# A third weight load split behind another step, and a norm's small products moved up by three and six products

## The chip, the cores and the metric

The kernel runs on one core of a Trainium2 chip. The metric is the device time of one execution in microseconds (us), the median of several. TensorE (PE) does matrix products, VectorE (DVE) and ScalarE (ACT) element-wise work, GpSimd (POOL) a little of it, and SyncE (SP) issues most of the DMA transfers.

## The reference

One transformer block over 512 tokens of width 1024, all in float32, batch and depth 1:

```
h  = rmsnorm(x)
z  = h @ W_in      # MLA q-latent 256 | MLA kv-latent 128 | rope key 32 | diff q, k, v 512 each
x += concat[8 MLA heads x 64, 4 differential heads x 128] @ W_out
x += W_down( silu(causal_dwconv3(h2 W_gate)) * (h2 W_up) ),   h2 = rmsnorm(x), width 2816
x += sigmoid(rmsnorm(x) W_pg) * (p W_pp)                       # p: 512 x 256
```

A differential head subtracts two softmax maps: `attn = probs[0] - lam * probs[1]`, each with a relative-position bias added to its logits. Attention is causal by chunks of 64 tokens.

## The kernel before

**Products.** Every product is three TensorE products, since a float32 number is split in a rounded high half and a low rest: `mm3` (L152 to L157) runs high by high (L155), high weight-low (L156 or L157), and low by high. Every weight is therefore loaded raw (`load_raw`, L140, by SyncE's queue), cast by ScalarE into its high half (L148) and subtracted by VectorE into its low half (L149); `load_w` does all three, and there are three raw buffers in the attention part. A raw buffer is free for the next load when the subtraction has read it.

**Order.** TensorE's instructions run in the order in which the code writes them. VectorE's and ScalarE's are placed by the framework's scheduler in the attention part, and in the order of the code from the FFN's preparation on (`region`, a manual schedule of VectorE, ScalarE and GpSimd). `tc.issue_after(ins)` tells the scheduler to put a block's VectorE instructions behind `ins`.

**Attention.** The MLA heads end in four outputs `yT0` to `yT3` (pairs of heads, 128 x 512), which `y_split` turns into `yh` (ScalarE, L183) and a low rest `yh0l` to `yh3l` (VectorE, L184); `df["ysplit"]` is the last such subtraction. W_out comes in tiles `o{kq}{dq}`: kq is 0 for the MLA half of its rows and 1 for the differential half, dq the quarter of its columns. `wo_units` feeds the MLA half's products between the differential heads' steps and adds each to x (L631). A differential step (`diff_logits`) writes logits `dl{head}{row block}{map}` to a bank (heads, blocks and maps counted from 0); VectorE adds the bias and takes the row minimum (L675), ScalarE takes the exponential with its sum (L676), and VectorE combines the two maps: a reciprocal (L680), the factor `cf` (L681), the map `pmd` (L682). At a head's end `mo` (L702) reads all four row sums.

**Between attention and FFN.** The last products of W_out end in x; its squares are summed by ScalarE, GpSimd and VectorE. TensorE meanwhile projects p in eight blocks (`pp_unit`, six products each). `norm_r` sums the squares over the rows with four tiny products (L925), takes the power -1/2 on GpSimd and writes a diagonal matrix on VectorE (L928); `norm_b` broadcasts it by one product (nrb, L932) that ScalarE copies (L933). From there `tokens` scales x into the FFN's input, one block `xg0` to `xg7` at each `next(tk)`: VectorE scales (L996) and subtracts the block ahead of it (L998), ScalarE casts (L1000). `pp_out` copies a block of p's projection out of its bank (ScalarE, L948) and sends it to DRAM. Each `next(w1)` prepares one weight of the FFN's second tile (cast L835, subtraction L839); the first tile's gate product `g0` takes the bank of the tag "tp" after `pp5`, and `u0` one of the tag "lg".

Of the kernel before, what the change touches and what calls it, by code (L numbers as in the profile page):

```python
# [21 lines left out]
T = 512  # L22
# [72 lines left out]
def hybrid_block(ctx: ExitStack, tc: tile.TileContext, a: dict, out: bass.AP):  # L95
# [13 lines left out]
    def bank(tag, name):  # L109
        return pp_.tile([P, 512], F32, tag=tag, bufs={"acc": 2, "lg": 3, "tp": 2, "ob": 1}[tag], name=name)  # L110
# [32 lines left out]
    def load_w(src, n, name, eng=None):  # L143

        raw = load_raw(src, n, name)
        hi = wp["pool"].tile([P, 1024], F32R, tag="hi", bufs=wp["w"], name=f"hi_{name}")
        lo = wp["pool"].tile([P, 1024], F32R, tag="lo", bufs=wp["w"], name=f"lo_{name}")
        S.copy(hi[:, :n], raw[:, :n])  # L148
        (eng or V).tensor_tensor(lo[:, :n], raw[:, :n], _f32(hi[:, :n]), op=ALU.subtract)  # L149
        return hi, lo  # L150

    def mm3(ps, blocks, first=True, last=True, again=False):  # L152
        n = len(blocks)
        for i, (xh, xl, wh, wl) in enumerate(blocks):
            TE.matmul(ps, xh, wh, start=first and i == 0, stop=False, skip_group_check=again)  # L155
            TE.matmul(ps, xh, wl, start=False, stop=False, skip_group_check=again)  # L156
            TE.matmul(ps, xl, wh, start=False, stop=last and i == n - 1, skip_group_check=again)  # L157

    def rms(y, ss, n, width):

        m = sm.tile([P, 32], F32, tag="rs_m", name="rs_m")[:, :n]
        V.tensor_scalar(m, ss, 1.0 / width, EPS, op0=ALU.mult, op1=ALU.add)
        G.tensor_tensor(y, m, mhalf[:, :n], op=ALU.pow)
# [84 lines left out]
    for kq in range(4):  # L248
# [12 lines left out]
        for j in range(2):  # L261
            k = 2 * kq + j
# [217 lines left out]
    for t in range(NT):  # L480
        kv_ = kvb[:, t]
        sqk = sq_tile("sqk")[:, :H * 64].rearrange("p (h d) -> p h d", d=64)
        for c in range(2):
            hs = slice(4 * c, 4 * c + 4)
            ps = bank(UP_BANKS[(2 * t + c) % 4], f"ukv{t}{c}")
# [18 lines left out]
    for t in range(NT):  # L504
        q_ = xn_tile(f"qn{t}")[:, :H * QK].rearrange("p (h d) -> p h d", d=QK)
        sq = sq_tile("sqq")[:, :H * QK].rearrange("p (h d) -> p h d", d=QK)
        for c in range(2):
            hs = slice(4 * c, 4 * c + 4)
            ps = bank(UP_BANKS[(2 * t + c) % 4], f"uq{t}{c}")
# [101 lines left out]
    yh, yl, df = [None] * 8, [None] * 8, {}  # L611
# [9 lines left out]
    def wo_blocks(k0, k1, b, w):  # L621

        c = [slice((k % 4) * 256 + (b % 2) * P, (k % 4) * 256 + (b % 2) * P + P) for k in range(k0, k1)]
        return [(w[0][:, c[i]], w[1][:, c[i]], yh[k0 + i], yl[k0 + i]) for i in range(k1 - k0)]
# [5 lines left out]
    def add_x(b, ps):  # L630
        V.tensor_tensor(xb(b), xb(b), ps, op=ALU.add)  # L631
# [3 lines left out]
    def wo_w(kq, dq):  # L635
        if (kq, dq) in wo_first:
            return wo_first.pop((kq, dq))
        return load_w(a["w_out"][kq, dq], 1024, f"o{kq}{dq}")

    def wo_units(kq, dqs, nk):  # L640

        for dq in dqs:
            w = wo_w(kq, dq)
            if kq:
                wo2[dq] = w
            for b in (2 * dq, 2 * dq + 1):
                ps = bank("acc", f"o{kq}{b}")
                for k in range(0, nk, 2):
                    mm3(ps, wo_blocks(4 * kq + k, 4 * kq + k + 2, b, w), k == 0, k == nk - 2)
                    if k == nk - 2:  # L650
                        add_x(b, ps)
                    yield
# [158 lines left out]
    ptw, wpp = (pk[:, 0], pk[:, 1]), [(pk[:, 2], pk[:, 3])]  # L811
# [90 lines left out]
    for b in order:  # L902
        if b in early:
            ps = early[b]
            mm3(ps, wo_blocks(7, 8, b, wo2[b // 2]), False, True)
        else:
            ps = bank("tp" if b == 3 else "lg", f"o3{b}")
# [13 lines left out]
    def norm_r():  # L921

        ss, ps = nrm["ss"], bank("ob", "nr")
        for t in range(NT):
            TE.matmul(ps[:, t:t + 1], ss[:, tsl[t]], ones[:, :1], start=True, stop=True)  # L925
        r4 = sm.tile([P, NT], F32, tag="r4", name="r4")
        rms(r4, ps[:, :NT], NT, D)
        V.tensor_tensor(nrm["dg"].rearrange("p (t q) -> p t q", t=NT), ident.unsqueeze(1).broadcast_to([P, NT, P]), r4.unsqueeze(2).broadcast_to([P, NT, P]), op=ALU.mult)  # L928

    def norm_b():  # L930
        ps = bank("ob", "nrb")
        TE.matmul(ps, ones, nrm["dg"], start=True, stop=True)  # L932
        S.copy(nrm["r"], ps)  # L933
# [3 lines left out]

    ppo = {}

    def pp_unit(b):  # L940
        ps, w = bank(("acc", "acc", "lg", "lg", "lg", "tp", "tp", "acc")[b], f"pp{b}"), wpp[b // 4]
        c = [slice(k * T + (b % 4) * P, k * T + (b % 4) * P + P) for k in range(2)]
        mm3(ps, [(w[0][:, c[k]], w[1][:, c[k]], ptw[0][:, k * T:k * T + T], ptw[1][:, k * T:k * T + T]) for k in range(2)])
        ppo[b] = ps

    def pp_out(b):
        o = t5("ppo")
        S.copy(o, ppo.pop(b))  # L948
        nc.sync.dma_start(pps[b], o)
# [69 lines left out]
    tk, w1 = tokens(), w_plain(1)  # L1019
    s0 = hi_(raw_w(gu(0, 2, 4), "rS", 0, bufs=3), "wS", 0)  # L1020
    for b in range(3):
        pp_unit(b)
    norm_r()
    for b in range(2):
        pp_out(b)
    for b in range(3, 5):
        pp_unit(b)
    W[0][1] = lo_(*s0)
    pp_out(2)
    next(w1)  # L1030
    norm_b()
    next(tk)
    pp_out(3)
    for b in range(4, 8):
        if b < 7:
            pp_unit(b + 1)
        next(tk)
        pp_out(b)
    for _ in tk:
# [283 lines left out]
    for b in (6, 7):  # L1323
        ps = bank("lg", f"dn4{b}")
# [27 lines left out]
    ps = [pg_bank(b) for b in range(4)]  # L1352
# [101 lines left out]
```

## Time and profile before

| what | value |
|---|---|
| three runs | 651.58 us median (650.05, 651.58, 651.68) |
| profiled execution, its own time | 649.71 us |
| its span in the trace | 647.9 us |
| granted TensorE clock, mean of the span | 0.998 of full speed |
| TensorE busy | 639.4 us, 99% of the span, 3916 instructions |
| VectorE busy | 481.3 us, 74% |
| ScalarE busy | 361.8 us, 56% |
| GpSimd busy | 55.5 us, 9% |
| DMA moved | 82.63 MB, mean 128 GB/s |

The span is what the trace covers; the profiled execution's time has 1.8 us outside of it. Busy time counts an engine's instructions, also those that overlap their neighbours: a TensorE product of 512 columns is listed with 0.39 us and follows its neighbour after 0.23.

### The profile page before, as it was taken

The numbers are of one execution on the slowest core, as the hardware profiler recorded it, in microseconds if no ns is written. First come the engines' busy times: TensorE is split into PE (matmuls) and PEld (weight loads), VectorE is DVE, ScalarE is ACT, GpSimd is POOL, SyncE is SP. The second block draws the span as 40 slices with busy tenths as digits, with TensorE's granted clock in tenths as the row PEclk, the third lists the DMA queues.
The fourth block names the chain that finished last, engine by engine and source line by source line (L and its number), as shares of the span: only waits on it lengthen the run. The fifth ranks groups of instructions, "written<-read, shape, count | busy, mean of one in ns | idle before, by whom it ended". The sixth has DMA issues, their size and how long they took to land.

```text
span 647.9 us, 10246 instructions
## 1 busy us (share of the span) xinstructions
PE 639.4 (99%) x3916; PEld 567.8 (88%) x3916; DVE 481.3 (74%) x870; ACT 361.8 (56%) x630; POOL 55.5 (9%) x92
## 2 busy tenths in 40 slices
PE   9999999999999999999999999999999999999997
PEld 9988888888687887889999999999999999988886
DVE  6889587646988767888876767676767677759844
ACT  7887566556676465657554555455454545637211
POOL 1510040000000121000100000000010000000000
PEclk9999999999999999999999999999999999999999
DMA  8241224130510158536774646564646464531121
GB/s 298 103 163 50 81 79 167 34 119 20 175 46 2 65 181 257 163 67 179 195 212 114 180 117 184 129 188 114 180 114 178 115 178 114 180 130 54 37 89 50
DMA packets 29912, 82.63 MB, mean 128 GB/s; under 512 B 3100, under 2 KB 4124, under 8 KB 29736
## 3 DMA queue, kind: packets, MB, share of 16 engines
q1 hardware_dynamic: 23816, 69.17, 31.7%
q0 software_dynamic: 5616, 12.33, 10.5%
q8 instruction: 31, 0.51, 0.3%
q10 hardware_dynamic: 432, 0.49, 0.2%
q14 instruction: 17, 0.14, 0.1%
HBM read 77.77 MB, written 5.52 MB: 129 GB/s over the span
## 4 chain that ended last, share of the span: by engine, by line
PE 91%; DVE 5%; ACT 3%; issue 1%; ACTq 0%
PE dn L157 6%; PE dn L156 6%; PE dn L155 6%; PE gx L157 4%; PE gx L155 4%; PE gx L156 4%; PE zd L155 3%; PE zd L157 3%; PE zd L156 3%; PE g L155 3%; PE g L156 3%; PE g L157 3%; PE o L155 3%; PE mo L583 2%; PE o L156 2%; PE pg L157 2%
## 5 line engine op out<-in xcount | busy, mean ns | idle before, releaser
L839 DVE TENSOR_TENSOR wSl<-rS,wSh 128x1024 fp32r<-128x1024 f32 x21 | 25.7, 1224 | 44.6 <-ACT wSh L835 44.5
L157 PE MATMUL dn<-ah,lo_dn 128*128 128x512 f32 x144 | 56.5, 392 | 0.0
L156 PE MATMUL dn<-al,hi_dn 128*128 128x512 f32 x144 | 56.4, 392 | 0.0
L155 PE MATMUL dn<-ah,hi_dn 128*128 128x512 f32 x144 | 56.0, 389 | 0.0
L956 POOL DMA_DIRECT2D rS<-in_w_gu x19 | 22.7, 1194 | 250.4 <-DVE cv L1124 124.7
L835 ACT CAST wSh<-rS 128x1024 fp32r<-128x1024 f32 x21 | 22.1, 1050 | 35.9 <-PE gy L156 35.6
L155 PE MATMUL zd<-hi_d,xh 128*128 128x512 f32 x96 | 39.5, 411 | 0.0
L156 PE MATMUL zd<-lo_d,xh 128*128 128x512 f32 x96 | 37.6, 391 | 0.0
L631 DVE TENSOR_TENSOR x<-x,dn 128x512 f32<-128x512 f32 x44 | 29.9, 680 | 6.5 <-PE dn L157 6.3
L839 DVE TENSOR_TENSOR wTl<-rA,wTh 128x1024 fp32r<-128x1024 f32 x19 | 23.3, 1225 | 15.0 <-ACT wTh L835 14.5
L573 ACT ACTIVATE pm<-ml,nm,rq 128x128 f32<-128x128 f32 (+3 forms) x32 | 19.8, 618 | 22.2 <-DVE nm L571 22.1
L157 PEld LDWEIGHTS dn<-ah,lo_dn 128*128 128x128 f32 x144 | 27.0, 188 | 5.6
L155 PEld LDWEIGHTS dn<-ah,hi_dn 128*128 128x128 f32 x144 | 27.1, 189 | 5.2
L156 PEld LDWEIGHTS dn<-al,hi_dn 128*128 128x128 f32 x144 | 27.0, 188 | 5.3
L570 DVE TENSOR_REDUCE nm<-ml 128x1 f32<-128x128 f32 (+3 forms) x32 | 15.6, 487 | 18.4 <-PE ml L157 18.3
L155 PE MATMUL o<-yh,hi_o 128*128 128x512 f32 x64 | 26.9, 421 | 0.6 <-ACT yh L183 0.6
L1127 ACT ACTIVATE cv<-cv 128x512 f32<-128x512 f32 x22 | 13.9, 631 | 23.9 <-DVE cv L1124 23.8
L155 PE MATMUL g<-b2h,wAh 128*128 128x256 f32 (+1 forms) x88 | 26.4, 300 | 0.2
L835 ACT CAST wAh<-rA 128x1024 fp32r<-128x1024 f32 x21 | 22.1, 1051 | 8.0 <-DMA rA<-in_w_gu 8.0
L839 DVE TENSOR_TENSOR wAl<-rA,wAh 128x1024 fp32r<-128x1024 f32 x21 | 25.6, 1217 | 1.2 <-ACT wAh L835 1.2
L156 PE MATMUL g<-b2l,wAh 128*128 128x256 f32 (+1 forms) x88 | 26.2, 298 | 0.0
L157 PE MATMUL g<-b2h,wAl 128*128 128x256 f32 (+1 forms) x88 | 26.2, 298 | 0.0
(478 smaller groups left out, 2221.2 us busy)
## 6 DMA issues: line engine op xcount, KB each, us to landing
rA<-in_w_gu SPq DMA_DIRECT2D x22, 512.0 KB, 3.9
rS<-in_w_gu SPq DMA_DIRECT2D x22, 512.0 KB, 3.5
rS<-in_w_gu POOLq DMA_DIRECT2D x19, 512.0 KB, 5.8
raw_dn<-in_w_down SPq DMA_DIRECT2D x18, 512.0 KB, 5.8
raw_d<-in_w_d SPq DMA_DIRECT2D x12, 512.0 KB, 3.3
r<-in_w_gu SPq DMA_DIRECT2D x19, 256.0 KB, 6.6
raw_o<-in_w_out SPq DMA_DIRECT2D x8, 512.0 KB, 3.5
rS_pg<-in_w_pg SPq DMA_DIRECT2D x6, 512.0 KB, 4.1
```

What stands on the lines that cost most here:

```text
L155: TE.matmul(ps, xh, wh, start=first and i == 0, stop=False, skip_group_check=again)
L156: TE.matmul(ps, xh, wl, start=False, stop=False, skip_group_check=again)
L157: TE.matmul(ps, xl, wh, start=False, stop=last and i == n - 1, skip_group_check=again)
L570: V.reduce_max(nm, ps[:, :n], axis=AX.X, negate=True)
L573: S.activation(pm[:, :n], ps[:, :n], AF.Exp, bias=nm, scale=r, accum_out=mla["ssum", h // 2][:, t, h % 2:h % 2 + 1])
L583: TE.matmul(po[:, w], pt[:, tsl[j]], kv[j][:, h, 96:], start=j == 0, stop=j == t)
L631: V.tensor_tensor(xb(b), xb(b), ps, op=ALU.add)
L835: S.copy(h_, src)
L839: V.tensor_tensor(l_, src, _f32(h_), op=ALU.subtract)
L956: nc.gpsimd.dma_start(sums[f].rearrange("p (i c) -> p i c", i=2), a["w_gu"][f][:, :2048].rearrange("p (i c) -> p i c", i=2)[:, :, :512], a ...
L1127: S.activation(cv, cv, AF.Silu)
```

## The change

Three edits. First, the weight tile (0,2), the third set of W_out's MLA half, is split behind the subtraction of the fourth MLA output. Second, `pp_unit` can run something between its two halves, and `norm_r` runs between the halves of block 2 and no longer behind block 2. Third, the calls that follow stand in another order: `norm_b` behind block 3 instead of behind block 4, the copies one place earlier against the projection's blocks, and the first `next(w1)` behind the copy of block 4 instead of ahead of `norm_b`.

```diff
     def wo_units(kq, dqs, nk):
         for dq in dqs:
-            w = wo_w(kq, dq)
+            with tc.issue_after(df["ysplit"].ins) if (kq, dq) == (0, 2) else ExitStack():
+                w = wo_w(kq, dq)
...
-    def pp_unit(b):
+    def pp_unit(b, mid=None):
         ps, w = bank(("acc", "acc", "lg", "lg", "lg", "tp", "tp", "acc")[b], f"pp{b}"), wpp[b // 4]
         c = [slice(k * T + (b % 4) * P, k * T + (b % 4) * P + P) for k in range(2)]
-        mm3(ps, [(w[0][:, c[k]], w[1][:, c[k]], ptw[0][:, k * T:k * T + T], ptw[1][:, k * T:k * T + T]) for k in range(2)])
+        for k in range(2):
+            mm3(ps, [(w[0][:, c[k]], w[1][:, c[k]], ptw[0][:, k * T:k * T + T], ptw[1][:, k * T:k * T + T])], k == 0, k == 1)
+            if k == 0 and mid:
+                mid()
         ppo[b] = ps
...
     for b in range(3):
-        pp_unit(b)
-    norm_r()
+        pp_unit(b, norm_r if b == 2 else None)
     for b in range(2):
         pp_out(b)
-    for b in range(3, 5):
-        pp_unit(b)
+    pp_unit(3)
     W[0][1] = lo_(*s0)
     pp_out(2)
+    norm_b()
+    pp_out(3)
+    next(tk)
+    pp_unit(4)
+    next(tk)
+    pp_out(4)
     next(w1)
-    norm_b()
-    next(tk)
-    pp_out(3)
-    for b in range(4, 8):
-        if b < 7:
-            pp_unit(b + 1)
+    for b in range(5, 8):
+        pp_unit(b)
         next(tk)
         pp_out(b)
```

Lines from `wo_units` on carry a number one higher after the change, and those from `pp_unit`'s body on four higher.

At the fourth MLA output VectorE runs before the change, from the low half of weight (0,2) on (`lo_o02`; `pmd_1916` is the 256-wide map of head 0, row block 1; `dl020` and `dl021` are the logits of head 0, row block 2):

```order
L149 TENSOR_TENSOR lo_o02_2239<-raw_o02_2236,hi_o02_2238 128x1024
L680 RECIPROCAL cf_1928<-s1_1911 128x1
L184 TENSOR_TENSOR yh3l_1952<-yT3_1946,yh3_1951 128x512
L681 SCALAR_TENSOR_TENSOR cf_1928<-cf_1928,nlam_221,s0_1881 128x1
L149 TENSOR_TENSOR lo_o03_2396<-raw_o03_2393,hi_o03_2395 128x1024
L682 SCALAR_TENSOR_TENSOR pmd_1916<-pmd_1924,cf_1928,pmd_1916 128x256
L631 TENSOR_TENSOR x0_1840<-x0_1840,o00_1939 128x512
L675 ISA pmd_1968,nmd_1969<-dl021_1964,strip_1095 128x384
L675 ISA nmd_1969 128x1
L149 TENSOR_TENSOR lo_o10_2529<-raw_o10_2526,hi_o10_2528 128x1024
```

and after it, from the same place (behind the bias step of `dl020`):

```order
L681 RECIPROCAL cf_1928<-s1_1911 128x1
L682 SCALAR_TENSOR_TENSOR cf_1928<-cf_1928,nlam_221,s0_1881 128x1
L683 SCALAR_TENSOR_TENSOR pmd_1916<-pmd_1924,cf_1928,pmd_1916 128x256
L184 TENSOR_TENSOR yh3l_1952<-yT3_1946,yh3_1951 128x512
L676 ISA pmd_1968,nmd_1969<-dl021_1964,strip_1095 128x384
L676 ISA nmd_1969 128x1
L149 TENSOR_TENSOR lo_o02_2239<-raw_o02_2236,hi_o02_2238 128x1024
L681 RECIPROCAL cf_1972<-s1_1955 128x1
L631 TENSOR_TENSOR x0_1840<-x0_1840,o00_1939 128x512
L682 SCALAR_TENSOR_TENSOR cf_1972<-cf_1972,nlam_221,s0_1881 128x1
```

`lo_o02` has moved behind `yh3l` and the bias step of `dl021`, the last two of the three small steps on `pmd_1916` have moved ahead of `yh3l`, and `lo_o10` has left this stretch for a place ahead of `lo_o11`, behind `mo`.

TensorE runs before the change, from the third product of block 2 of p's projection on:

```order
L157 MATMUL pp2_2853<-pk_2673 128x512
L155 MATMUL pp2_2853<-pk_2673 128x512
L156 MATMUL pp2_2853<-pk_2673 128x512
L157 MATMUL pp2_2853<-pk_2673 128x512
L925 MATMUL nr_2860<-ones_77,nr0_2751 128x1 x4
L155 MATMUL pp3_2876<-pk_2673 128x512
```

and after it:

```order
L157 MATMUL pp2_2853<-pk_2673 128x512
L926 MATMUL nr_2857<-ones_77,nr0_2751 128x1 x4
L155 MATMUL pp2_2853<-pk_2673 128x512
L156 MATMUL pp2_2853<-pk_2673 128x512
L157 MATMUL pp2_2853<-pk_2673 128x512
L155 MATMUL pp3_2876<-pk_2673 128x512
```

The four sums of the norm stand three products sooner. In the same way `nrb` stands behind block 3 now, six products sooner, and nothing else of TensorE's order is moved.

ScalarE runs before the change, from the copy of the second block on (`wAh1` is the cast of the next FFN weight, `nr1` the copy of the broadcast, `b1h` the casts of the token blocks):

```order
L948 COPY ppo_2873<-pp1_2846 128x512
L948 COPY ppo_2891<-pp2_2853 128x512
L835 CAST wAh1_2896<-rA_1_2894 128x1024
L933 COPY nr1_2752<-nrb_2900 128x512
L1000 CAST b1h_2828<-xg0_2903 128x512
L948 COPY ppo_2906<-pp3_2876 128x512
L1000 CAST b1h_2828<-xg1_2916 128x512
L948 COPY ppo_2920<-pp4_2883 128x512
L1000 CAST b1h_2828<-xg2_2930 128x512
```

and after it:

```order
L952 COPY ppo_2873<-pp1_2846 128x512
L952 COPY ppo_2884<-pp2_2853 128x512
L934 COPY nr1_2752<-nrb_2887 128x512
L952 COPY ppo_2890<-pp3_2876 128x512
L1004 CAST b1h_2828<-xg0_2893 128x512
L1004 CAST b1h_2828<-xg1_2903 128x512
L952 COPY ppo_2907<-pp4_2896 128x512
L836 CAST wAh1_2912<-rA_1_2910 128x1024
L1004 CAST b1h_2828<-xg2_2923 128x512
```

The copy of the broadcast stands where `wAh1` stood, and `wAh1` stands behind the copy of block 4, between the second and third token block. VectorE's subtraction `wAl1` has moved with it, from ahead of `xg0` to behind `xg1` and `b1l` of block 0, ahead of `xg2`.

## Rows read from the trace of the kernel before

**Rows 1.** The whole execution: first the page's line of engines (busy time, share of the span, instructions), then TensorE's waits that bear on the two places (released by: us in total, times, longest).

```profile
PE 639.4 (99%) x3916; PEld 567.8 (88%) x3916; DVE 481.3 (74%) x870; ACT 361.8 (56%) x630; POOL 55.5 (9%) x92
...
PE o L155 <- ACT yh L183: 0.6, 1, 0.6
PE g L155 <- ACT ppo L948: 0.5, 1, 0.5
PE o L156 <- DVE yh3l L184: 0.4, 1, 0.4
```

**Rows 2.** TensorE (PE) in order of time around the fourth MLA output's products: start us, duration us, engine, line, operation, out<-in, shapes, and in brackets the idle time before it with its releaser.

```profile
165.06 0.40 PE L157 MATMUL o<-yh,lo_o 128*128 128x512 f32 x1
166.07 0.50 PE L155 MATMUL o<-yh,hi_o 128*128 128x512 f32 x1 [0.62 <-ACT yh L183]
167.01 0.50 PE L156 MATMUL o<-yh3l,hi_o 128*128 128x512 f32 x1 [0.43 <-DVE yh3l L184]
167.35 0.39 PE L157 MATMUL o<-yh,lo_o 128*128 128x512 f32 x1
```

**Rows 3.** VectorE (DVE) in order of time at the same place, then ScalarE (ACT) there.

```profile
165.07 1.22 DVE L149 TENSOR_TENSOR lo_o<-raw_o,hi_o 128x1024 fp32r<-128x1024 f32 x1
...
166.21 0.16 DVE L680 RECIPROCAL cf<-s 128x1 f32<-128x1 f32 x1
166.28 0.67 DVE L184 TENSOR_TENSOR yh3l<-yT,yh 128x512 fp32r<-128x512 f32 x1
...
165.37 0.19 ACT L676 ACTIVATION_READ_ACCUMULATOR pmd<-pmd,nmd 128x1 f32 x1
```

**Rows 4.** VectorE further on: the small steps of one combination of two probability maps, its first row and the row that follows its third.

```profile
179.33 0.16 DVE L680 RECIPROCAL cf<-s 128x1 f32<-128x1 f32 x1
...
180.18 0.55 DVE L675 CUSTOM_DVE_ANT_0 pmd<-dl,strip 128x384 f32<-128x384 f32 x1
```

**Rows 5.** The load of w_out's second set (1,1) and what stands behind it: its issue on SyncE's queue (SP); from the view of the tile raw_o over 155 to 175 us the time from issue to landing; ScalarE's cast of that load and the end of the exponential behind it (of head 0, row block 3); VectorE's next bias step and the split of head 2's queries; TensorE's first product of them.

```profile
166.36 0.33 SPq L140 DMA_DIRECT2D raw_o<-in_w_out  x1
...
DMA to landing us min/median/max: 3.5/4.3/4.9
...
171.96 1.05 ACT L148 CAST hi_o<-raw_o 128x1024 fp32r<-128x1024 f32 x1 [0.97 <-PE o L156]
...
173.54 0.19 ACT L676 ACTIVATION_READ_ACCUMULATOR pmd<-pmd,nmd 128x1 f32 x1
...
175.72 0.28 DVE L675 CUSTOM_DVE_ANT_0 pmd<-dl,strip 128x128 f32<-128x128 f32 x1
...
184.70 0.75 DVE L187 SCALAR_TENSOR_TENSOR st<-d0T,dcol,st 128x512 fp32r<-128x512 f32 x1
...
185.84 0.33 PE L155 MATMUL dl<-st 64*128 64x128 f32 x2
```

**Rows 6.** TensorE between the projection of p and the FFN: the product that stands fourth in block 2, the second norm's sums (nr) and its broadcast (nrb), the last product of block 7, the first two gate products.

```profile
241.54 0.39 PE L155 MATMUL pp<-pk 128*128 128x512 f32 x1
...
242.22 0.94 PE L925 MATMUL nr<-ones,nr 128*128 128x1 f32 x8
...
245.89 1.02 PE L932 MATMUL nrb<-nr,ones 128*128 128x512 f32 x2
...
250.65 0.39 PE L157 MATMUL pp<-pk,wTlpp 128*128 128x512 f32 x1
251.56 0.50 PE L155 MATMUL g<-b1h,wAh 128*128 128x512 f32 x1 [0.52 <-ACT ppo L948]
251.90 0.39 PE L156 MATMUL g<-b1l,wAh 128*128 128x512 f32 x1
```

**Rows 7.** VectorE at that place: the last add of the second norm's squares, the diagonal (nr), a weight's low half (wAl), the first two scaled token blocks (xg).

```profile
240.65 0.69 DVE L897 TENSOR_TENSOR nr<-nr,nsq 128x512 f32<-128x512 f32 x1 [0.16 <-ACT nsq L890]
...
244.50 0.69 DVE L928 TENSOR_TENSOR nr<-ident,r 128x512 f32<-128x512 f32 x1 [1.13 <-POOL r L163]
...
246.24 1.22 DVE L839 TENSOR_TENSOR wAl<-rA,wAh 128x1024 fp32r<-128x1024 f32 x1
247.58 1.42 DVE L996 SCALAR_TENSOR_TENSOR xg<-x,cols,nr 128x512 f32<-128x512 f32 x2
```

**Rows 8.** ScalarE at that place: a weight's cast (wAh), the copy of the broadcast, a token block's cast, a block's copy.

```profile
242.90 1.06 ACT L835 CAST wAh<-rA 128x1024 fp32r<-128x1024 f32 x1
246.95 0.59 ACT L933 COPY nr<-nrb 128x512 f32<-128x512 f32 x1 [2.99 <-PE nrb L932]
...
250.40 0.62 ACT L1000 CAST b1h<-xg 128x512 fp32r<-128x512 f32 x1
250.93 0.58 ACT L948 COPY ppo<-pp 128x512 f32<-128x512 f32 x1
```

**Rows 9.** Where the first gate bank is used: TensorE's step over its next wait, VectorE's and ScalarE's first steps of the convolution.

```profile
285.57 0.39 PE L157 MATMUL u<-b2h,wSl 128*128 128x512 f32 x1
286.04 0.39 PE L155 MATMUL g<-b2h,wAh 128*128 128x256 f32 x1
...
263.37 0.74 DVE L1123 SCALAR_TENSOR_TENSOR cv<-g,cols,cv 128x511 f32<-128x511 f32 x1
...
262.14 0.78 ACT L1119 ACTIVATE cv<-g,cols 128x512 f32<-128x512 f32 x1 [1.67 <-issue]
```

**Rows 10.** Busy time of each engine in 163 to 169 us, with TensorE's granted clock (PEclk, share of full speed).

```profile
163.00:169.00 6.00, 4.95 (x25) 3.26 (x24) 5.58 (x13) 4.28 (x9) 0.00 (x0) 1.00 0.55 173
```


## The prediction made before the changed kernel ran

> **What bounds the kernel now.** The line of engines [rows 1] has TensorE busy for 639.4 of 647.9 us, so only a gap of TensorE can give time. I then read its waits: two of them lie at the fourth MLA output (0.6 on the cast `yh`, 0.4 on `yh3l`), one at the first gate product (0.5 on `ppo`). The change touches these two places alone.
>
> How much they cost is read from TensorE's steps. Three products of 512 columns take 242.22 − 241.54 = 0.68 us, 0.23 each [rows 6]. At the first place the steps are 1.01, 0.94 and 0.34 [rows 2]; less 0.23 each, the loss is 0.78 + 0.71 + 0.11 = 1.60 us, the last part being a slow step behind a wait. At the second place the last product ahead starts at 250.65, the gate product at 251.56, the next at 251.90 [rows 6]: 0.68 + 0.11 = 0.79 lost. The ceiling of any gain is therefore 2.4 us, 0.37% of 651.58. Times differ from no change by a measurable amount from about 0.3% on, which is 1.95 us here.
>
> **Part A, weight (0,2).** *What is taken away.* The low half `lo_o02` stood on VectorE at 165.07, and `yh3l` began at 166.28 when it was over [rows 3]. It now stands behind `yh3l`. The cast `yh`, which releases the first wait, is ScalarE's and its order ahead of it is unchanged, so the first 0.78 stays.
>
> *What takes its place.* The three small steps of a map's combination now stand ahead of `yh3l`. The first is a reciprocal of a row sum that ScalarE delivers at 165.37 + 0.19 = 165.56 [rows 3], so it begins at 165.6. The steps take 180.18 − 179.33 = 0.85 [rows 4]; `yh3l` begins at 166.45 in place of 166.28, and TensorE is **0.17 late**. The other bound is that `yh3l` begins as soon as TensorE's first product shows its cast to be done, at 166.07 [rows 2]: 0.2 early. I take the late one, since the order is fixed and the row sum's end is in a row.
>
> *What is late next.* The raw buffer. The load of weight (1,1) was issued at 166.36 [rows 5], just behind the end of `lo_o02` (165.07 + 1.22 = 166.29). Now `yh3l` runs from 166.45 for 0.67 [rows 3], the bias step of `dl021` takes 0.55 behind it [rows 4], less some 0.15 in which neighbours overlap, and `lo_o02` runs from 167.5 to 168.74. The load goes out at 168.8, 2.45 later. From issue to landing these loads take 3.5, 4.3 or 4.9 [rows 5]. I take 3.5, since the loads behind it move by the same 2.45 and so keep their distance: it lands at 172.3. ScalarE's cast of it stood at 171.96 [rows 5], so ScalarE is 0.35 late (1.75 with 4.9). Behind the cast on ScalarE stands the exponential of head 0's last row block; from the cast's start to that step's end is 173.54 + 0.19 − 171.96 = 1.77. VectorE's `mo` waits for that row sum, until 172.3 + 1.77 = 174.1. Behind `mo` now stand `lo_o10`, a reciprocal, `lo_o11` and another reciprocal, and only then the bias step that stood at 175.72 [rows 5]. A subtraction steps on by 166.21 − 165.07 = 1.14 and a reciprocal by 0.07 [rows 3]; `mo` is as small as the latter. 174.1 + 0.07 + 2 × 1.21 = 176.6: **0.9 late**. VectorE is never idle for long enough between there and the split of head 2's queries at 184.70 to make that up, by its order; the split then ends at 184.70 + 0.9 + 0.75 = 186.35. TensorE's first product of it stood at 185.84, without a wait [rows 5], and would come at 186.01 by the 0.17. So it waits, and is **0.5 late** in all; that 0.5 contains the 0.17. Part A is +0.5, from −0.2 (the early `yh3l`, the load hidden) to +1.9 (4.9 to land, 1.4 more).
>
> On these loads the Trainium skill, "DMA: Bandwidth & Descriptors", section "Issuing engines are not separate DMA queues", says that all transfers run on the same 16 DMA engines and interleave, whoever started them. By it a later load meets what is then under way and may take the 4.9, and part A would be +1.9; by the row it takes 3.5 and part A is +0.5. No row of before shows the load at its new place.
>
> **Part B, norm and copies.** *The gain.* The squares' sum is ready at 240.65 + 0.69 = 241.34 [rows 7], so the four sums can run at 241.54, where block 2's fourth product stood, in place of 242.22 [rows 6]: 0.68 earlier. The diagonal ends at 244.50 + 0.69 − 0.68 = 244.51 [rows 7]. TensorE comes to the broadcast six products sooner, at 245.89 − 6 × 0.23 = 244.51 [rows 6]: just in time, about 244.56, without a new wait worth naming and **1.33 earlier**.
>
> *What it meets.* The copy of the broadcast comes at 246.95 − 1.33 = 245.62 [rows 8], the first two token blocks run from 247.58 − 1.33 = 246.25 to 247.67 (1.42 for both) [rows 7]. Their casts on ScalarE follow, the second at 247.7, and a cast and the copy behind it are 0.53 apart [rows 8]: the copy of block 4 at 248.2. Here the weight's cast `wAh1` now stands. It took 1.06 at 242.90, in a stretch in which ScalarE then waited 2.99 for the broadcast [rows 8]: it cost nothing there. That cover is gone: it runs from 248.7 to 249.8. Its subtraction on VectorE takes 1.22 [rows 7], from 249.8 to 251.0, with the third token block queued behind it: 251.0 to 251.7 (half of 1.42). ScalarE's third cast waits for that, and behind the cast stands the copy of block 5, at 251.7 + 0.53 = 252.25, ending 252.85 (0.58 long). That copy frees the bank of the first gate product. TensorE has nothing else and is free at 250.65 + 0.23 = 250.88: it waits 2.0 where it lost 0.68, and the gate product is at 252.9 in place of 251.56, **1.3 late**.
>
> *What comes back.* TensorE's next gap is at 286.04: a step of 0.47 in place of 0.23 [rows 9], and 0.11 for the slow step behind a gap as at 167.35. I put it down to VectorE, which forms the sums of token halves that this product reads. Its convolution chain, which stands among them, begins with the first convolution step at 263.37, while ScalarE's step on the same bank ends at 262.14 + 0.78 = 262.92: 0.45 of slack. So VectorE is late by 1.3 − 0.45 = 0.9 when TensorE is late by 1.3, and the gap of about 0.35 at 286.04 closes. Part B is **+0.9**. Its ends: +1.4, nothing back, and +0.4, when later gaps give back as much once more.
>
> Costed at nothing: the move of an FFN weight load behind three small stores on SyncE's queue, whose weight is used two FFN tiles later; the loads (1,2) and (1,3) some 2.5 to 5 us later, whose weights stand behind the queries of head 2.
>
> **The sum.** +0.5 + 0.9 = +1.4 on the profiled execution: 649.71 + 1.4 = 651.1. The median of the runs is 1.87 above that execution, so on its scale the time is 651.58 + 1.4 = 653.0, within 0.3% of before.
>
> **The rivals.**
>
> *The gain as it stands in the order (faster).* The earlier broadcast lets the copies run one place sooner, block 5's bank is free by 250.88 and the gap of 0.79 goes; `yh3l` is 0.2 early. That is −1.0: 650.6, still within 0.3%. For it speaks the 1.33; against it that `wAh1` and its subtraction, 1.06 and 1.22, now lie between the second and the third token block. It decides where the copy of block 5 ends 2.0 us sooner than worked out. Chance 0.12.
>
> *The raw buffer decides (slower).* The mechanism is the load of (1,1): from a landing time of 4.1 on, the extra 0.55 carries the sum over +1.95; at 4.9 it is +1.4 more, +2.8: 654.4. For it speaks that two of three figures in the view lie above 4.1; against it that the same load took 3.5 with the same neighbours. Chance 0.18.
>
> *The late gate product is hidden.* VectorE and ScalarE run ahead of TensorE through the FFN, later gaps give back nearly all of part B, and part A alone is left: +0.5, 652.1. For it speaks the 0.45 of slack; against it that TensorE is busy 99% and has few gaps. Chance 0.12.
>
> *The clock falls.* Over 163 to 169 the granted clock was 1.00 although TensorE was busy for only 4.95 of 6.00 [rows 10]; a stop of 2.0 us right behind full work is longer than the gaps seen there. If the clock fell to the lower level, 1.2 for 2.4 GHz, each 0.23 step would take 0.46 until it rises; no row tells until when, and for the 12 products of the first two gate and up blocks it would add 2.8: 655.8. Chance 0.03.
> The Trainium skill, "TensorE: Matmul & The Clock Gate", Part 1, says that the throttled state is the default and activity releases it; rows 10 show no fall.
>
> **How the numbers follow.** The forecast has 0.55; its own range is 652.0 to 653.9 (part A −0.2 to +0.9 and part B as above, not both at an end). The range, 650.6 to 655.0, takes in the gain, the hidden delay and most of the raw buffer's case. Slower by over 0.3% is above 653.53: the raw buffer 0.18, the clock 0.03, and the upper fifth of the forecast, 0.12: 0.33. Faster by over 0.3% is below 649.63, more than the gain's case gives: 0.04 for an earlier `yh` besides. Within: 0.63.
>
> **What would show it.** In the profile of the changed kernel: `yh3l` at about 166.45 and TensorE's product of it 0.17 late; the load of (1,1) at 168.8; VectorE's bias step of head 1 at 176.6 and a wait of TensorE of some 0.3 near 186 that was not there; the broadcast at 244.56 without a wait; `wAh1` at 248.7, in the middle of the token blocks; a wait for `ppo` of about 2 us ahead of the first gate product; the gap at 286 gone. The prediction is wrong if the copy of block 5 ends before 251, if the first product at 166.07 moves, or if the later FFN waits change by more than 0.5.

## The result and the profile after

The changed kernel takes 652.27 us in the median of 20 executions (650.99 to 654.53), the kernel before 650.29 in 20 beside them (648.89 to 651.68): a ratio of 1.003 with a 95% interval of 1.0022 to 1.0039, **2.0 us slower**. The forecast was +1.4 us with a range of −1.0 to +3.4. The profiled execution of the changed kernel has a span of 650.3 us. One execution of e4 (892.67 us) and one of the kernel before beside it (780.57 us), slow at a granted clock of 0.655 and 0.754, are left out of all ratios and counts below.

The page's line of engines, and TensorE's three longest waits away from the start, which answer to [rows 1]:

```profile
PE 639.5 (98%) x3916; PEld 566.2 (87%) x3916; DVE 481.2 (74%) x870; ACT 361.9 (56%) x630; POOL 55.3 (9%) x92
...
PE g L155 <- ACT ppo L952: 1.8, 1, 1.8
...
PE o L156 <- DVE yh3l L184: 0.6, 1, 0.6
PE o L155 <- ACT yh L183: 0.6, 1, 0.6
```

TensorE's work is the same to 0.1 us. Its wait ahead of the first gate product has gone from 0.5 to 1.8; that for `yh3l` from 0.4 to 0.6, and the one for `yh` has stayed.

To see where the 2.4 us between the two spans arise, the start of each TensorE product was compared with the same product's start before (positive is late). The profiled execution is 0.67 late already at 162 us, where nothing is changed: it lost that in the first 12 us, where its first products wait 0.4 and 0.3 for the two halves of the first weight. From the first product of `yh` on, it goes like this:

| stretch (times of before) | late | of it new |
|---|---|---|
| first product of `yh`, 166.07 | +0.61 | |
| behind the product of `yh3l`, 167.3 to 168.2 | +0.78 | +0.17 |
| behind head 2's first queries, 188 to 192 | +1.31 | +0.53 |
| p's projection, 247.3 to 250.8 | +1.52 | +0.21 |
| first gate and up products, 253 to 258 | +2.80 | +1.28 |
| from 310 to the end | +2.38 | −0.42 |

Part A is +0.70, part B is +1.07.

At the first place, VectorE of the changed kernel in order of time, from the reciprocal ahead of `yh3l` to the split of head 2's queries, which answers to [rows 3] and [rows 5]:

```profile
166.19 0.16 DVE L681 RECIPROCAL cf<-s 128x1 f32<-128x1 f32 x1 [0.37 <-ACT pmd L677]
...
167.05 0.69 DVE L184 TENSOR_TENSOR yh3l<-yT,yh 128x512 fp32r<-128x512 f32 x1
...
174.66 0.16 DVE L703 SCALAR_TENSOR_TENSOR mo<-s 128x4 f32<-128x4 f32 x1 [0.17 <-ACT pmd L677]
...
177.20 0.28 DVE L676 CUSTOM_DVE_ANT_0 pmd<-dl,strip 128x128 f32<-128x128 f32 x1
...
179.16 0.68 DVE L631 TENSOR_TENSOR x<-x,o 128x512 f32<-128x512 f32 x1
179.76 0.42 DVE L676 CUSTOM_DVE_ANT_0 pmd<-dl,strip 128x256 f32<-128x256 f32 x1
...
180.92 0.16 DVE L681 RECIPROCAL cf<-s 128x1 f32<-128x1 f32 x1 [0.73 <-ACT pmd L677]
...
182.12 0.68 DVE L184 TENSOR_TENSOR st<-d1T,st 128x512 fp32r<-128x512 f32 x1
182.72 0.55 DVE L676 CUSTOM_DVE_ANT_0 pmd<-dl,strip 128x384 f32<-128x384 f32 x1
...
184.12 0.17 DVE L681 RECIPROCAL cf<-s 128x1 f32<-128x1 f32 x1 [0.83 <-ACT pmd L677]
...
186.38 0.74 DVE L187 SCALAR_TENSOR_TENSOR st<-d0T,dcol,st 128x512 fp32r<-128x512 f32 x1
```

The same steps of the kernel before (the reciprocal of the first pair is the 179.33 of [rows 4]):

```profile
178.16 0.42 DVE L675 CUSTOM_DVE_ANT_0 pmd<-dl,strip 128x256 f32<-128x256 f32 x1
...
178.51 0.68 DVE L631 TENSOR_TENSOR x<-x,o 128x512 f32<-128x512 f32 x1
...
180.66 0.55 DVE L675 CUSTOM_DVE_ANT_0 pmd<-dl,strip 128x384 f32<-128x384 f32 x1
...
181.23 0.69 DVE L184 TENSOR_TENSOR st<-d1T,st 128x512 fp32r<-128x512 f32 x1
182.43 0.16 DVE L680 RECIPROCAL cf<-s 128x1 f32<-128x1 f32 x1 [0.51 <-ACT pmd L676]
```

The reader is to see four waits in the changed kernel, 0.37, 0.17, 0.73 and 0.83. The first two were worked out ahead; the last two were not. At 179.16 an addition of 0.68 stands *ahead* of a bias step, and the reciprocal that needs the exponential of that step waits for it at 180.92 with nothing long between; before, the addition stood between the two. In the same way the split of head 1's keys (182.12) now stands ahead of a bias step (182.72) and stood behind it. The change's wait on one subtraction made the scheduler place these later steps otherwise as well.

At the second place, TensorE, ScalarE and VectorE of the changed kernel, which answers to [rows 6 to 8]:

```profile
245.98 1.10 PE L933 MATMUL nrb<-nr,ones 128*128 128x512 f32 x2
...
252.17 0.39 PE L157 MATMUL pp<-pk,wTlpp 128*128 128x512 f32 x1
254.35 0.50 PE L155 MATMUL g<-b1h,wAh 128*128 128x512 f32 x1 [1.80 <-ACT ppo L952]
...
249.71 0.58 ACT L952 COPY ppo<-pp 128x512 f32<-128x512 f32 x1
250.19 1.05 ACT L836 CAST wAh<-rA 128x1024 fp32r<-128x1024 f32 x1
253.19 0.62 ACT L1004 CAST b1h<-xg 128x512 fp32r<-128x512 f32 x1 [1.96 <-DVE xg L1000]
253.72 0.58 ACT L952 COPY ppo<-pp 128x512 f32<-128x512 f32 x1
...
251.27 1.23 DVE L840 TENSOR_TENSOR wAl<-rA,wAh 128x1024 fp32r<-128x1024 f32 x1 [1.40 <-ACT wAh L836]
252.41 0.75 DVE L1000 SCALAR_TENSOR_TENSOR xg<-x,cols,nr 128x512 f32<-128x512 f32 x1
```

This is the chain as it was forecast, link by link: cast 250.19, subtraction 251.27, third token block 252.41, its cast 253.19, copy of block 5 to 254.30, gate product 254.35. VectorE waits 1.40 for the cast and ScalarE then 1.96 for VectorE: the two engines take turns, and for the last 1.80 of it TensorE stands still.

### The profile page after: what moved, and what is told of

Its sections match the earlier page's. It is cut to its first block, busy times and chain, and to the rows that moved or that the text cites. A ratio compares the mean times of both kernels' runs of the same rounds, so it can differ in the third digit from the quotient of the medians.

```text
span 650.3 us, 10247 instructions
## 1 busy us (share of the span) xinstructions
PE 639.5 (98%) x3916; PEld 566.2 (87%) x3916; DVE 481.2 (74%) x870; ACT 361.9 (56%) x630; POOL 55.3 (9%) x92
## 4 chain that ended last, share of the span: by engine, by line
PE 89%; DVE 4%; ACT 3%; DMA 2%; issue 1%; ACTq 0%; SPq 0%
PE dn L157 6%; PE dn L156 6%; PE dn L155 6%; PE gx L157 4%; PE gx L155 4%; PE gx L156 4%; PE g L155 4%; PE g L156 4%; PE g L157 4%; PE zd L155 3%; PE zd L157 3%; PE zd L156 3%; PE pg L157 2%; PE pg L155 2%; PE pg L156 2%; PE mo L583 2%
```

## The experiments

Each ratio is against the kernel before, run beside it on the same chip. Lateness is again TensorE's against the profiled execution of before; it is read over a stretch, since an execution's start alone moves it by up to 1 us, and e1 and e8 lose 0.65 and 1.25 more between 100 and 120 us, where their order is that of before. Lines that only note an instruction in `df` or in a list are left out of the edits shown.

**Part A alone, e1.**

```diff
-            w = wo_w(kq, dq)
+            with tc.issue_after(df["ysplit"].ins) if (kq, dq) == (0, 2) else ExitStack():
+                w = wo_w(kq, dq)
```

> The kernel before with the first edit alone: weight (0,2) split behind the fourth MLA output. My theory (part A costs by itself: the row sum's wait ahead of yh3l, then VectorE late through the later load and the two subtractions behind mo): TensorE 0.1 to 0.2 late at the product of yh3l, a stop at the first product of head 2's queries that was not there before, 0.6 late behind it, nothing changed at the first gate product; ratio 1.0009 (+0.6 us). Rival (the whole loss of the changed kernel is part B's): no stop at head 2's queries, ratio 1.0000 or below.

Measured 1.0019 (1.0005 to 1.0032): 651.08 against 650.00. TensorE is 0.28 late at the product of `yh`, 0.45 behind `yh3l` and 1.27 behind head 2's first queries: +0.99. VectorE waits 0.34, 0.45, 0.73 and 0.83 where the changed kernel has 0.37, 0.17, 0.73 and 0.83; the load of (1,1) took 3.7 us here and 3.4 there. The rival is out: part A costs by itself. This profile loses 0.48 more from 258 to 290 us, where the code is that of before and ScalarE's copies of p's last blocks wait for stores to land. The last of them, in the kernel before and here:

```profile
256.37 0.59 ACT L948 COPY ppo<-pp 128x512 f32<-128x512 f32 x1 [0.80 <-DMA pps<-ppo]
...
258.15 0.59 ACT L949 COPY ppo<-pp 128x512 f32<-128x512 f32 x1 [1.39 <-DMA pps<-ppo]
```

ScalarE is 1.78 late behind it and TensorE 1.75 from 286 on. e8 has 1.76 for the same wait and loses there in the same way (+0.87 to +1.72), although part A's loss is gone there; the changed kernel and e2 have no such wait. Why these stores land later was not tested, so the profile's end is no measure of part A.

**Part B alone, e2.** The changed kernel with the edit above taken back.

```diff
-            with tc.issue_after(df["ysplit"].ins) if (kq, dq) == (0, 2) else ExitStack():
-                w = wo_w(kq, dq)
+            w = wo_w(kq, dq)
```

> The kernel before with the edits to p's projection, the norm and the order of the calls alone. My theory: the broadcast 1.2 us earlier, the cast wAh1 between the casts of the second and third token block, a wait of about 1.8 us for the copy of block 5 ahead of the first gate product, TensorE 1.3 late there, about 0.3 given back at the first step of 256 columns near 286: ratio 1.0016 (+1.0 us). Rival (the two parts work on each other, since part A's lateness is what makes part B late): no wait above 1 us at the first gate product, ratio within 1.0005.

Measured 1.0009 (0.9999 to 1.0019): 650.92 against 650.00, so the runs alone would leave it open, and the size is little over half of what was expected. The profile does not leave it open: no lateness up to p's projection (−0.01), a wait of 1.8 for the copy ahead of the gate product. This profile shows something more, TensorE behind that wait, in order of time, and the busy time of the engines in three stretches with the granted clock (the third figure from the end):

```profile
250.84 0.39 PE L157 MATMUL pp<-pk,wTlpp 128*128 128x512 f32 x1
253.02 0.61 PE L155 MATMUL g<-b1h,wAh 128*128 128x512 f32 x1 [1.79 <-ACT ppo L951]
253.43 0.63 PE L156 MATMUL g<-b1l,wAh 128*128 128x512 f32 x1
253.85 0.63 PE L157 MATMUL g<-b1h,wAl 128*128 128x512 f32 x1
...
256.77 0.39 PE L155 MATMUL u<-b1h,wSh 128*128 128x512 f32 x1
257.00 0.40 PE L156 MATMUL u<-b1l,wSh 128*128 128x512 f32 x1
```

```profile
247.00:253.00 6.00, 4.22 (x19) 3.17 (x17) 4.57 (x7) 3.78 (x6) 0.00 (x0) 1.00 1.04 305
253.00:257.00 4.00, 3.98 (x11) 3.13 (x11) 4.00 (x8) 2.92 (x6) 0.00 (x0) 0.57 0.91 358
257.00:263.00 6.00, 6.00 (x28) 4.95 (x27) 5.28 (x9) 2.11 (x3) 0.00 (x0) 1.00 0.44 129
```

Behind the wait the products follow each other by 0.42 in place of 0.23, nine of them, and the granted clock is 0.57 over 4 us, the lower level for most of it. TensorE is 1.46 late at the gate product and 3.03 late nine products on: the clock cost 1.6 us in this execution. The changed kernel's profile has the same wait and no such stretch. That is the rival of the falling clock, come true in this execution, the slowest of the 12; less that 1.6, TensorE ends 1.07 late, as much as part B costs in the changed kernel's profile.

**Part B with the weight step back, e3.**

```diff
     pp_out(2)
+    next(w1)
     norm_b()
...
     pp_out(4)
-    next(w1)
```

> As the run before (part B alone), but the first weight step, which casts wAh1 and subtracts wAl1, back at its place ahead of the norm's broadcast; the norm's sums, the broadcast and the copies stay where the change put them. My theory (the weight step in the middle of the token blocks is the whole cost): the cast lies in ScalarE's idle time ahead of the broadcast's copy, the subtraction delays the first token block by some 0.4, the copy of block 5 ends ahead of the last product of block 7, and the first gate product comes without a wait: TensorE 0.6 to 0.8 earlier there than before, part of it given back; ratio 0.9990 (-0.6 us). Rival (the cost lies in the norm's earlier products or in the copies' new places): a wait of over 1 us at the first gate product remains, ratio 1.001 or more.

Measured 0.9976 (0.9968 to 0.9985): 648.79 against 650.00, **faster than before**, by twice what was expected. TensorE, ScalarE and VectorE of this kernel at the second place:

```profile
250.97 0.39 PE L157 MATMUL pp<-pk,wTlpp 128*128 128x512 f32 x1
251.20 0.39 PE L155 MATMUL g<-b1h,wAh 128*128 128x512 f32 x1
...
243.93 1.05 ACT L835 CAST wAh<-rA 128x1024 fp32r<-128x1024 f32 x1
245.91 0.59 ACT L933 COPY nr<-nrb 128x512 f32<-128x512 f32 x1 [0.94 <-PE nrb L932]
...
245.69 1.22 DVE L839 TENSOR_TENSOR wAl<-rA,wAh 128x1024 fp32r<-128x1024 f32 x1
246.82 1.41 DVE L999 SCALAR_TENSOR_TENSOR xg<-x,cols,nr 128x512 f32<-128x512 f32 x2
```

The cast lies in ScalarE's wait for the broadcast, which is still 0.94 long behind it, and the gate product follows the last product of block 7 without a gap. TensorE goes from +0.12 to −0.50 there and to −0.92 by 310, since the gaps near 286 and 289 shrink too. So the earlier norm and the copies are worth 1.0 us of the profile; the weight step among the token blocks turned that into a loss of 1.1. The rival is out.

**Both gaps at the first place taken away, e4.** The cast of (0,3) is held behind that of the fourth output, on the kernel before. The instruction named is ScalarE's here, and it is the block's ScalarE cast that is held.

```diff
-            w = wo_w(kq, dq)
+            with tc.issue_after(df["ycast"].ins) if (kq, dq) == (0, 3) else ExitStack():
+                w = wo_w(kq, dq)
```

> The kernel before with another edit at the first place: the cast of weight (0,3) on ScalarE is held behind the cast of the fourth MLA output, so that this one comes about 1 us sooner; VectorE's subtraction of the output then comes ahead of lo_o02 by itself. Both of TensorE's waits there should go: 1.4 us earlier at the second block of products. Theory 1 (a gap of TensorE is worth its length): ratio 0.998 (-1.4 us). Theory 2 (VectorE sets the pace of the differential heads, so that what TensorE gains it waits for later): TensorE stops at head 2's queries for 0.7 and again behind them, and the ratio is between 0.9995 and 1.0008.

Measured 0.9992 (0.9982 to 1.0002): 649.78 against 650.00. Both waits are gone and TensorE is 1.6 earlier behind them (from −0.30 to −1.90), but behind head 2's first queries it stands at −0.45: nearly all is given back. Where, VectorE and ScalarE show, then TensorE:

```profile
180.32 0.56 DVE L680 CUSTOM_DVE_ANT_0 pmd<-dl,strip 128x384 f32<-128x384 f32 x1
...
182.36 0.16 DVE L685 RECIPROCAL cf<-s 128x1 f32<-128x1 f32 x1 [1.47 <-ACT pmd L681]
...
180.51 1.05 ACT L813 CAST pk<-raw_pT 128x1024 fp32r<-128x1024 f32 x1 [0.65 <-DMA raw_pT<-in_pT]
...
185.43 0.32 PE L157 MATMUL dl<-st 64*128 64x128 f32 x1 [0.68 <-DVE st L189]
```

ScalarE waits for a load that is not needed for 50 us, casts it, and only then takes the exponential for which VectorE waits 1.47. Theory 1 is out; the ratio lies just below the range that theory 2 gave, and its interval takes in no change. The ceiling of 2.4 us in the prediction counted 1.6 us of gaps at the first place that are worth little by themselves: before, VectorE's split of head 2's queries ends only 0.39 ahead of TensorE (185.45 against 185.84 [rows 5]), so TensorE can gain no more than that unless the split comes sooner; in e4 it comes 0.2 later.

**Part A with another buffer, e5,** to take the late load away and keep every order.

```diff
+        if name == "o10":
+            raw = kv_tile("raw_o10").rearrange("p t h d -> p (t h d)")[:, :1024]
+        else:
             raw = wp["rawpool"].tile([P, 1024], F32, tag="raw", bufs=wp["raw"], name=f"raw_{name}")
```

> Part A alone, with one raw buffer more: weight (1,0) is loaded into the memory of the MLA keys, which nothing uses any more, so that the load of (1,1) waits for an earlier subtraction and no longer for lo_o02. Every engine's order is that of part A alone. Theory 1 (the late load of (1,1) is what costs): the load goes out near 163.5 and not at 169, VectorE does not wait at mo, TensorE has no new stop at head 2's queries and is 0.1 to 0.2 late there, from yh3l alone; ratio 1.0003. Theory 2 (VectorE's new order costs, with two subtractions in a row behind mo and a wait ahead of yh3l): TensorE stops at head 2's queries as with part A alone, 0.6 to 1.0 late; ratio 1.001 to 1.002.

Measured 1.0015 (1.0004 to 1.0027): 650.60 against 649.82. The load of (1,1) goes out at 162.17 and VectorE no longer waits at `mo`, but two of its other waits are unchanged:

```profile
179.18 0.42 DVE L679 CUSTOM_DVE_ANT_0 pmd<-dl,strip 128x256 f32<-128x256 f32 x1
...
180.34 0.16 DVE L684 RECIPROCAL cf<-s 128x1 f32<-128x1 f32 x1 [0.73 <-ACT pmd L680]
...
183.54 0.16 DVE L684 RECIPROCAL cf<-s 128x1 f32<-128x1 f32 x1 [0.83 <-ACT pmd L680]
```

TensorE goes from +0.15 to +0.32 behind `yh3l` and to +0.74 behind head 2's queries: +0.59, against +0.99 in e1 and +0.70 in the changed kernel. The load is a part of it, some 0.1 to 0.4, and no more; theory 1 falls.

**The two long steps back, e8,** on top of e5.

```diff
+        with tc.issue_after(df["bias", 1, 1, 1].ins) if b == 2 and ("bias", 1, 1, 1) in df and not wo2 else ExitStack():
             V.tensor_tensor(xb(b), xb(b), ps, op=ALU.add)
```

> As part A alone with the other buffer, and the addition of o02 to x held behind the bias step of head 1's row block 1, where it stood before the change; with it the scheduler puts the split of head 1's keys back behind the bias step of row block 2 as well. Theory 1 (part A costs because these two long VectorE steps no longer lie between a bias step and the reciprocal that waits for its exponential): VectorE's waits of 0.73 and 0.83 at the two reciprocals fall to 0.2 to 0.5 together, TensorE is no more than 0.25 late behind head 2's first queries, ratio 1.0003. Theory 2 (the two subtractions in a row behind mo are the cost, wherever the small steps stand): 0.5 late or more there, ratio 1.001 or above.

Measured 1.0003 (0.9992 to 1.0015): 649.98 against 649.97. VectorE at the same two reciprocals:

```profile
179.42 0.42 DVE L680 CUSTOM_DVE_ANT_0 pmd<-dl,strip 128x256 f32<-128x256 f32 x1
...
179.77 0.68 DVE L635 TENSOR_TENSOR x<-x,o 128x512 f32<-128x512 f32 x1
180.59 0.17 DVE L685 RECIPROCAL cf<-s 128x1 f32<-128x1 f32 x1
...
183.55 0.17 DVE L685 RECIPROCAL cf<-s 128x1 f32<-128x1 f32 x1 [0.47 <-ACT pmd L681]
```

The addition lies behind the bias step, its 0.68 covers the exponential, and the first shows no wait (0.13 us of idle time is left, as before); the second is 0.47. TensorE goes from +0.74 at the product of `yh` to +0.91 behind `yh3l` and is at +0.87 behind head 2's queries: only the 0.17 of `yh3l` is left. Theory 1 holds. The two subtractions behind `mo` still make the next bias step 0.47 late, but 0.09 of it is left at the split of head 2's queries and nothing of it reaches TensorE.

**The gap at the gate product filled, e6.** Eight products that nobody reads, in the changed kernel.

```diff
+        if f == 0:
+            fps = bank("ob", "fillps")
+            for _ in range(8):
+                TE.matmul(fps, ptw[0][:, :P], ptw[0][:, :T], start=True, stop=True)
```

> The changed kernel with 8 products of 512 columns more, which nobody reads, ahead of the first gate product, where TensorE stands still for 2 us. Theory 1 (the clock falls behind that stop in some executions, and that is part of the measured loss): the gate product begins within 0.1 us of the changed kernel's time, no execution shows a mean granted clock of 0.997 or less, and the ratio falls from 1.003 to 1.002 (+1.1 to +1.4 us). Theory 2 (the low clocks have nothing to do with the stop): a third of the executions still shows 0.997 or less, and the ratio stays at 1.003.

Measured 1.0046 (1.0031 to 1.0061) in only 6 executions, 650.95 to 654.48. The gap is filled and the gate product comes as late as in the changed kernel (1.30 behind p's projection, 1.27 there). None shows a mean clock of 0.997 or less, as theory 1 has it, but the time did not fall, against theory 1. With two executions above 653 at a clock of 0.999 the spread has another source, and **the run settles nothing about the time**.

**Two subtractions to GpSimd, e7,** on top of e4.

```diff
-        return load_w(a["w_out"][kq, dq], 1024, f"o{kq}{dq}")
+        return load_w(a["w_out"][kq, dq], 1024, f"o{kq}{dq}", G if (kq, dq) in ((0, 3), (1, 0)) else None)
```

> As the run with the cast of weight (0,3) held behind the cast of the fourth MLA output, and the low halves of (0,3) and (1,0) subtracted by GpSimd, which is idle there, in place of VectorE (2 x 1.22 us less on VectorE). Theory 1 (VectorE sets the pace between 165 and 186 us): what TensorE gains at the fourth output is no longer given back at head 2's queries: ratio 0.998 (-1.4 us). Theory 2 (the pace is set by the chain of bias, exponential and combination over three engines, or GpSimd holds up the loads behind it): given back as before or worse: ratio 0.9992 or above.

Measured 1.0015 (1.0006 to 1.0024): 650.81 against 649.82, a miss for theory 1. GpSimd and VectorE in order of time:

```profile
165.70 5.77 POOL L149 TENSOR_TENSOR lo_o<-raw_o,hi_o 128x1024 fp32r<-128x1024 f32 x2 [60.33 <-ACT hi_o L148]
...
166.62 2.61 DVE L687 SCALAR_TENSOR_TENSOR pmd<-pmd,cf 128x256 f32<-128x256 f32 x1
```

A VectorE step of two 128x256 maps took 2.61 here, where it takes 0.48 (e4, the same row). So the run does not test what VectorE's load is worth: it put a new stop in its way, and the obvious next test, less work on VectorE without GpSimd, was not run.

**ScalarE's casts of p held back, e9,** on top of e4.

```diff
-        S.copy(pk[:, 2 * i], raw)
+        with tc.issue_after(df["exp", 2, 1].ins):
+            S.copy(pk[:, 2 * i], raw)
```

> As the run with the cast of weight (0,3) held behind the fourth output's cast (all on VectorE again), and ScalarE's two casts of p's tiles, which wait for their loads in the middle of head 1, held behind an exponential of head 2. Theory 1 (the gain at the fourth output was given back because the cast of p waited 0.65 for its load and took 1.05, and held the exponential that VectorE waited 1.47 for): that wait falls below 0.5, TensorE is still about 1.0 early behind head 2's first queries and at the end, ratio 0.9986 (-0.9 us). Theory 2 (VectorE's work alone sets the pace from 165 to 186): early by less than 0.4 there, ratio 0.9995 or above.

Measured 0.9991 (0.9976 to 1.0005): 649.20 against 649.97, between the theories and not clear of no change. VectorE's wait of 1.47 is 0.83, a new one of 0.39 lies at 173.83, and TensorE keeps 0.8 of the 1.6 (+0.46 ahead, −1.14 behind the fourth output, −0.30 behind head 2's queries). By the end 0.50 of it is left. The cast of p is a part of what took the gain back; that the bare length of bias, exponential and reciprocal is the rest is read from the 0.83, not tested.

**All that gains, e10.** e9 and e3 together.

> The run before together with part B with the first weight step back at its place: what the two gained apart should add, since one lies ahead of 187 us and the other behind 240: ratio between 0.9955 and 0.9970 (-2.0 to -2.9 us). If VectorE or the loads of the FFN weights are the next limit behind 250, it is no lower than that of the second alone, 0.9976.

Measured 0.9964 (0.9951 to 0.9976): 647.95 against 649.97, 2.0 us faster than before, where the changed kernel is 2.0 us slower. What e3 and e9 gained apart (0.24% and 0.09%) adds up. Behind the start no wait of TensorE is longer than 0.3 now.

## Why the prediction came out

The side, the place and the mechanism of the larger part were right, and the sum was 0.6 us short. That the forecast time of 653.0 lies 0.7 from the measured 652.27 is luck: it stood on the median of three runs, 651.58, and the median of 20 is 650.29.

**The first product of `yh3l`.** Forecast 0.17 late, measured 0.17 in the changed kernel, e1, e5 and e8. The reason, a reciprocal that waits for its row sum, is the 0.37 in VectorE's row.

**The load and what stands behind it.** Less the 0.66 of the start, the load of (1,1) went out at 169.41 − 0.66 = 168.75 (forecast 168.8), took 3.4 (3.5), its cast began at 172.86 − 0.66 = 172.20 (172.3), `mo` at 174.0 (174.1), the bias step at 176.54 (176.6). Each link came as worked out. The late landing of 4.9 did not come.

**"0.9 late at the split of head 2's queries".** The size held (186.38 − 0.66 = 185.72 against 184.70: 1.0 late), and so did the 0.5 at TensorE within 0.2. The reason held in part. The step that failed is the sentence that VectorE is carried along from 176.6 to 184.70 "by its order": the order of that stretch was taken from before and only its start was moved. VectorE's lateness at the bias step behind `mo` and at the split, less that of TensorE at 162 us, and the time between the two steps:

| kernel | bias step late | from there to the split | split late |
|---|---|---|---|
| before | | 8.98 | |
| changed | 0.81 | 9.19 | 1.02 |
| e1 | 1.06 | 9.19 | 1.27 |
| e5 | 0.61 | 9.20 | 0.83 |
| e8 | 0.47 | 8.59 | 0.09 |

In the changed program's order the stretch is equally long whatever the lateness at its start, so all of that lateness is carried along, as forecast, and 0.2 is added. With the addition and the key split back behind their bias steps (e8) the same stretch is 0.6 shorter. VectorE is busy for 0.48 less in it than before (7.42 against 7.90), but idles 0.73 and 0.83 at the two reciprocals where it idled 0.14 and 0.13 around the first and 0.51 at the second. So both reach TensorE, the late load and the two moved steps: in e5 the wait at `mo` is gone and 0.59 remains; with the two steps moved back 0.13 remains. The late load with the two steps at their old places was not run; by these rows its split would be some 0.4 late, an estimate, about the 0.39 by which the split of before is ahead of TensorE. That the 0.9 came out is in part luck.

**The chain behind the broadcast.** Less the 1.32 with which TensorE came there, the cast `wAh1` began at 248.87 (forecast 248.7), the copy of block 5 ended at 252.98 (252.85), the gate product began at 253.03 (252.9). The weight step as the cause is shown by e3. Against the forecast 1.3, TensorE was 1.28 later in the first gate products than in p's projection, and 0.2 more came from the broadcast itself, costed at nothing "worth naming".

**What came back.** Forecast 0.35 to 0.4 near 286, measured 0.42. VectorE's first convolution step is 2.39 late where TensorE is 2.80 late, so the 0.45 of slack is there (0.41). Part B is then 1.07 for a forecast 0.9.

**The ceiling.** The 2.4 us of gaps were counted as if each were worth its length. At the first place e4 took away 1.6 of them, and 0.15 was left behind head 2's first queries. This did not touch the sum, but the bound was too generous.

**The rivals.** The gain as it stands was in the change and is what e3 measures; it failed at the place named for it, the weight step. The clock, given 0.03 and 2.8 us, deserved more chance and less price: of the changed kernel's 20 timed executions 8 have a mean granted clock of 0.997 or less, with a median of 653.2, and the other 12 have one of 651.4. So some 0.6 to 0.8 of the 2.0 us goes with the clock, and the other 12 stand 1.1 above the median of before. The sum left this to a rival. The changed kernel's profiled execution shows no low clock behind the wait and is 1.77 late by parts A and B all the same, 0.2 over the forecast in each, so the 0.6 is not the clock's alone. With part B's stop in the program (the changed kernel and e2) it is 10 of 32 executions; in e1, e3 to e10, without a stop of that length, 3 of 94, and 1 of 83 of the kernel before run beside them. That is a coincidence over many runs and one profile that shows the mechanism; e6, made to prove it, did not.

The Trainium skill, "TensorE: Matmul & The Clock Gate", Part 1, says that the throttled state is the default and that activity releases it. The profile of e2 agrees: 1.00 before the wait of 1.79, the lower level for nine products behind it, 1.00 again.

## What to carry to other kernels

When one step is held back, read the new order to the next place where the waiting engine is met, not only at the edit: a long step that used to lie between a short one and its answer is a cover, and a scheduler moves covers without notice. Before moving a chain earlier, list what was put in its idle time, since it has to go somewhere: the same cast cost nothing in ScalarE's wait of 2.99 and 1.3 us three places later. A gap of the busiest engine is worth its length only if the engines that feed it are ahead at the next meeting point.

## What the runs showed of the hardware

In e7 a GpSimd subtraction of 128x1024 took about 2.9 us (5.77 for two), where VectorE takes 1.22. A VectorE step with two inputs in on-chip memory, begun at 166.62 while the first of the two ran, took 2.61 in place of 0.48 and ended 0.3 behind the end of that subtraction. VectorE's own subtraction of two such inputs, begun at 165.48, 0.2 ahead of GpSimd's, took its usual 1.22, and the addition at 169.16, with one input from a bank, its 0.68. So the row looks like a wait for the step that began first, not like a general slowing. The Trainium skill, "GPSIMD Engine Reference", section "1. Specifications", has the two engines share their interfaces to that memory, with contention for VectorE steps of two such inputs; the row agrees and gives the price. And the same wait of 1.8 us was followed by the lower clock in one profiled execution and not in another, which puts 1.6 us between two executions of much the same code.
